# Moving the chain that finds the values' scale from the end of the projections to between the last query blocks

## The chip, the core and the metric

The kernel runs on one core of a Trainium2 chip. A core has a matrix engine (TensorE, PE in the profile), three engines for elementwise work (VectorE or DVE, ScalarE or ACT, GpSimd or POOL) and a queue engine (SyncE or SP) that starts transfers. Each engine takes its instructions in order, and the engines wait for one another at semaphores. The metric is the time of one execution in microseconds (us); lower is better.

## The reference

Two layers of an encoder on 1024 tokens of width 1024. A layer is attention with low-rank queries and values beside a convolution branch, then a gated feed-forward stage:

```python
h = _rmsnorm(x, g_mix[l])
p = h @ w_in[l]
c_q = _rmsnorm(p[..., :o1], g_q[l])
q = (c_q @ w_uq[l]).reshape(b, s, MLA_HEADS, MLA_NOPE_DIM + MLA_ROPE_DIM)
c_kv = _rmsnorm(p[..., o1:o2], g_kv[l])
kv = (c_kv @ w_ukv[l]).reshape(b, s, MLA_HEADS, MLA_NOPE_DIM + MLA_V_DIM)
k_nope, v = kv[..., :MLA_NOPE_DIM], kv[..., MLA_NOPE_DIM:]
y_attn = _mla_attention(q_nope, q_rope, k_nope, k_rope, v)
a, gt = jnp.split(p[..., o3:], 2, axis=-1)
u = jax.nn.silu(_layernorm(_dwconv(a * jax.nn.sigmoid(gt), w_dw_conv[l], b_dw_conv[l]), ...))
x = x + jnp.concatenate([y_attn, u], axis=-1) @ w_o[l]
z = _dwconv(_rmsnorm(x, g_ffn[l]) @ w_up[l], w_dw_ffn[l], b_dw_ffn[l])
zg, zv = jnp.split(z, 2, axis=-1)
x = x + (jax.nn.silu(zg) * zv) @ w_down[l]
```

There are 8 heads with 64 plain and 32 rotary query dimensions and 64 value dimensions. Everything is float32. The kernel splits each float32 operand into an upper and a lower part and multiplies three pairs of parts, so one product of 128 inner rows and 512 columns costs three matmuls.

## The kernel before, in words

A layer has three stages: the projections (`project`), attention (`attention`) and output projection with feed-forward (`feed`). Each stage opens its own pool of PSUM banks, and a bank of the new pool waits for the last reader of the same bank in the old one. The order of the instructions on each engine is written out by hand: what the Python code emits first stands first in the engine's queue.

`project` walks a list `seq` of blocks. For each block n it emits the block's matmuls (`emit`), then VectorE work that the planner has by then (`work`), then what the entry names as `after`, and then it puts the block's eviction on the planner's list (`launch`). The last entries are the query blocks `u0`, `u1` (rotary part) and `n0` to `n3` (plain part), 18 matmuls each, on three wide PSUM tiles in turn. The eviction of block j (`query`, L741 to L745) multiplies the product by the query's norm on VectorE (L741), casts the result to its upper part on ScalarE (L743), and takes the lower part on VectorE (L745); stores on SP's queue then put both parts into memory ("spills"), from which the later heads' operands are loaded again. Head 0 gets its operands straight from these tiles. The value weights `w["v"]` are cast by a transfer on GpSimd's queue; the lower part is made by a copy on ScalarE (L189) and an adding transfer (L190), emitted ahead of `n1`.

Scratch tiles come from a ring of 31 slots: each new tile takes the slot of the oldest, and its writer waits for that tile's last users, transfers among them.

The values are stored as two 16-bit parts, so they need a scale. It is found by a short chain:
- `value_squares`: two ScalarE activations (L860) square the weighted upper value weights, one for each half of the 256 latent rows, and sum each along its row into a column of the small tile `vf`;
- `value_scale`: two matmuls with a matrix of ones (L868) add these columns over the rows into one PSUM tile, and three VectorE operations on a column (L870 to L872) make from the sum's exponent the scale `vs` and its inverse `vr`.

In this kernel `value_squares` is emitted in the return statement of `project`, behind the last eviction, and `value_scale` is the first thing that `attention` emits.

`attention` then emits the value rows: `rows(tt)` makes six matmuls for 128 tokens (L1538), and its eviction makes the upper part on ScalarE (L1548) and the lower on VectorE (L1551), both with `vs`. Three such blocks come first, then scores of query block 0 (L1562), block 3, scores of query block 1, blocks 4 and 5, and then scores of query block 2, which stands where the first of the two score tiles must have been emptied by the exponential (L1572), which needs the maximum from VectorE (L1564). From there each step has scores, transposes of the exponentials (L1602), their eviction (L1604, L1605) and the product with the values (L1625). Beside it GpSimd makes late taps of the convolution (L1794 to L1799) from an agenda by step; at the end it adds up the convolution's channels (L1805), and the first matmul behind the last product with the values is that of the convolution's norm (`lnp`, L1821).

Of the kernel before, what the change touches and what calls it, by code (L numbers as in the profile page):

```python
# [25 lines left out]
QL = 384  # L26
# [99 lines left out]
class Encoder:  # L126
# [421 lines left out]
    def project(self, l, carry):  # L548
# [3 lines left out]
        taps, active, u, conv, away, far_at = [], [], {}, {}, {}, {}  # L552
        gates, ckv, kvs, cq, cqs, vs, w = {}, [], [], [], [], [], {}
        heads, pending, spills = {}, {}, []
        qd = [self.dp.tile([HEADS, NOPE, T], F32R, name=f"qd{l}{i}") for i in range(2)]
        qrd = [self.dp.tile([2, HEADS, HALF, T], F32R, name=f"qrd{l}{i}") for i in range(2)]
        kd = [self.dp.tile([HEADS, NOPE, T], F32R, name=f"kd{l}{i}") for i in range(2)]
        krd = [self.dp.tile([ROPE, T], F32R, name=f"krd{l}{i}") for i in range(2)]
        st = {}

        def work(until):
            while True:
                at = next((e for e in active if e[0] <= clock["dve"]), None)
                if at is None and taps and clock["dve"] + TAP <= until:
                    j, t = taps.pop(0)
                    self.conv_step(l, j, u[j], conv[j], t)
                    clock["dve"] += TAP
                    continue
                if at is None:
                    at = min(active, key=lambda e: e[0], default=None)  # L570
                    if at is None or at[0] > until:
                        return
                    clock["dve"] = max(clock["dve"], at[0])
                step = next(at[1], None)
                if step is None:
                    active.remove(at)
                else:
                    clock["dve"] += step[0]
                    at[0] = clock["dve"] + step[1]

        def launch(steps, n=-1):
            active.append([clock["pe"], steps, n])
# [130 lines left out]
        def query_rope(i):  # L713
            p = ps[f"u{i}"]
            c, s = self.blk(f"rc{l}_{i}"), self.blk(f"rs{l}_{i}")
            nc.vector.tensor_tensor(out=c, in0=p, in1=st["cos"], op=ALU.mult)
            nc.vector.tensor_tensor(out=s, in0=p, in1=st["sin"], op=ALU.mult)
            st["rope", i] = c, s
            yield 2.44, 0.0
            if i == 0:  # L720
                return
            (c1, s1), (c2, s2) = st.pop(("rope", 0)), st.pop(("rope", 1))
            nc.vector.tensor_tensor(out=c1, in0=c1, in1=s2, op=ALU.subtract)
            nc.vector.tensor_tensor(out=c2, in0=c2, in1=s1, op=ALU.add)
            his = [self.blk(f"qr{l}_{i}", F32R) for i in range(2)]
            for hi, o in zip(his, (c1, c2)):
                nc.scalar.copy(out=hi, in_=o)
            yield 2.5, 1.0
            for i, (hi, o) in enumerate(zip(his, (c1, c2))):
                nc.vector.scalar_tensor_tensor(out=o.bitcast(F32R), in0=o, scalar=1.0, in1=hi.bitcast(F32), op0=ALU.mult, op1=ALU.subtract)  # L730
                sp = hi, o.bitcast(F32R)
                yield 1.25, 0.0
                for p in range(2):
                    for h in range(DIRECT):
                        self.move(heads[h][0][p][NOPE + i * HALF:NOPE + (i + 1) * HALF, :],
                                  sp[p][h * HALF:(h + 1) * HALF, :])
                spills.extend((qrd[p][i].rearrange("h d t -> (h d) t"), sp[p]) for p in range(2))

        def query(j):
            n = self.blk(f"qn{l}_{j}")  # L740
            nc.vector.tensor_tensor(out=n, in0=ps[f"n{j}"], in1=st["rq"], op=ALU.mult)  # L741
            hi = self.blk(f"qns{l}_{j}", F32R)
            nc.scalar.copy(out=hi, in_=n)  # L743
            yield 1.22, 1.5
            nc.vector.scalar_tensor_tensor(out=n.bitcast(F32R), in0=n, scalar=1.0, in1=hi.bitcast(F32), op0=ALU.mult, op1=ALU.subtract)  # L745
            sp = hi, n.bitcast(F32R)
            for p in range(2):
                for e in range(DIRECT if j == 0 else 0):
                    self.move(heads[e][0][p][0:NOPE, :], sp[p][e * 64:(e + 1) * 64, :])
                spills.append((qd[p][2 * j:2 * j + 2].rearrange("h d t -> (h d) t"), sp[p]))  # L750
            while j and spills:
                self.move(*spills.pop(0))
            yield 1.25, 0.0
# [11 lines left out]
        def ranked(group, j, n, name, moving):  # L765
            def run():
                pair = tuple(t[:, j] for t in w[group])
                self.product(ps[name], lambda k: tuple(t[:, k * 128:(k + 1) * 128] for t in pair), moving)
            return run
# [20 lines left out]
        add = lambda name, weight, emit, evict, after=None: seq.append((name, weight, emit, evict, after))  # L790
# [19 lines left out]
        for i in range(2):  # L810
            held = lambda: launch(query_rope(0), len(seq) - 6)
            add(f"u{i}", "u2", ranked("u2", i, QL, f"u{i}", cqs), lambda i=i: query_rope(1) if i else iter(()), held if i else norm)
        for j in range(4):
            add(f"n{j}", f"u{j // 2}", ranked(f"u{j // 2}", j % 2, QL, f"n{j}", cqs), lambda j=j: query(j))

        times, starts, t = {}, {}, 0.0
        for name, weight, *_ in seq:
# [33 lines left out]
            launch(evict(), n)  # L851
        supply(clock["pe"])
        work(1e9)
        return u, conv, away, (qd, qrd, kd, krd), (kvs, w["v"], self.value_squares(l, w["v"])), heads

    def value_squares(self, l, w):
        f = self.cp.tile([128, 8], F32, name=f"vf{l}", tag="vf", bufs=1)
# [667 lines left out]
    def attention(self, l, u, conv, away, spill, kvs, loaded, ahead, wo, begun):  # L1525
# [2 lines left out]

        load = lambda h: self.load_head(l, h, *spill)
        state, v, vts = {}, [], {}  # L1530
        vs, vr = self.value_scale(l, kvs[2])

        def rows(tt):
            (kv, wv, _), ts = kvs, slice(tt * 128, (tt + 1) * 128)
# [153 lines left out]
        while any(rest.values()):  # L1688
            j = max((j for j in rest if rest[j]), key=lambda j: (all(j != e for e, _ in late[-2:]), len(rest[j]), -j))
# [3 lines left out]
        for i, (j, t) in enumerate(late):  # L1693
            n, steps = int(SIDE_TIME * sum(costs[:i]) / sum(costs)), self.tap_late(l, j, t, u[j], conv[j], kinds[i])
# [245 lines left out]
```

## Time and profile before

| | us |
|---|---|
| Median of 3 runs | 2290.26 |
| Lowest and highest | 2286.81, 2290.73 |
| Profiled execution, its own time | 2288.28 |
| Its span | 2286.5 |

| Engine | busy us | share of the span |
|---|---|---|
| TensorE | 2269.4 | 99% |
| VectorE | 1735.7 | 76% |
| ScalarE | 1298.6 | 57% |
| GpSimd | 781.9 | 34% |

The profile is one execution. A row of the timeline gives the start and the duration in us, the engine, the line of the kernel, the operation, what it writes and reads, and, in brackets, for how long the engine had been idle before it and whom it waited for. A row marked x6 stands for six instructions in sequence. The chain of work follows the work that ended last backward from its end. A row of waits names who waited for whom, the total in us, the number of times and the longest. A row of windows gives for a stretch of time the length, the busy time and number of instructions of each engine, the clock granted to TensorE (1.00 is full), the share of the transfer engines and GB/s. Lines are those of the kernel before; the change adds two lines above line 815, so later lines count two more after it.

### The profile page before, as it was taken

What the parts mean: (1) busy time and instruction counts of PE and PEld (TensorE: products, weight loads), DVE (VectorE), ACT (ScalarE), POOL (GpSimd) and SP (SyncE); (2) the same over time, 40 slices, a digit from 0 to 9 for tenths busy, and PEclk for the clock granted to TensorE, in tenths of its full rate; (3) what the DMA queues carried; (4) which work ended last, traced back from release to release, by engine and by line L of the source; (5) the groups of instructions that cost most, each with busy time, mean ns of one, the idle gap of its engine ahead of it and who ended that gap; (6) DMA issues with size and microseconds to landing.
All of it is one profiled execution on the core that took longest, in us unless ns stands there. A gap on an engine that the chain in (4) does not pass through costs nothing.

```text
span 2286.5 us, 30445 instructions
## 1 busy us (share of the span) xinstructions
PE 2269.4 (99%) x10690; PEld 1838.8 (80%) x10690; DVE 1735.7 (76%) x2305; ACT 1298.6 (57%) x2058; POOL 781.9 (34%) x812
## 2 busy tenths in 40 slices
PE   9999999999999999999999999999999999999998
PEld 8887777788888888888888877777888888888887
DVE  7988888868877776776559778887687777768765
ACT  5355977646655555544533468785466555555444
POOL 1221788522333333001412237964323333320032
PEclk9999999999999999999999999999999999999999
DMA  6887998846899998935968979977659999988356
GB/s 195 166 181 243 193 205 180 226 133 148 211 279 293 278 295 206 334 106 143 206 137 166 224 224 205 190 157 204 175 122 228 268 303 277 293 213 316 109 120 171
DMA packets 199145, 475.73 MB, mean 208 GB/s; under 512 B 27232, under 2 KB 35280, under 8 KB 198992
## 3 DMA queue, kind: packets, MB, share of 16 engines
q0 software_dynamic: 103136, 222.46, 48.5%
q1 hardware_dynamic: 95568, 250.80, 32.8%
q8 instruction: 84, 1.38, 0.2%
q14 instruction: 69, 0.57, 0.1%
q10 hardware_dynamic: 288, 0.53, 0.1%
HBM read 309.29 MB, written 80.40 MB: 170 GB/s over the span
## 4 chain that ended last, share of the span: by engine, by line
PE 88%; DVE 6%; DMA 2%; ACT 2%; issue 2%; POOL 0%; DVEq 0%; SPq 0%; POOLq 0%; ACTq 0%
PE p L1118 34%; PE pd L1306 18%; PE po L929 7%; PE s L1562 7%; PE t L1602 4%; PE o L1625 4%; PE pa L226 2%; PE pg L226 2%; DVE conv L1777 2%; PE pg L545 2%; PE pq L226 1%; PE pv L1538 1%; PE pkv L226 1%; PE pa L545 1%; PE pn L226 1%
## 5 line engine op out<-in xcount | busy, mean ns | idle before, releaser
L1118 PE MATMUL p<-b,w 128*128 128x512 f32 x3552 | 806.9, 389 | 0.3 <-DVE w L1497 0.2
L1118 PEld LDWEIGHTS p<-b,w 128*128 128x128 f32 x3552 | 666.2, 188 | 140.3 <-DVE w L1497 1.0
L1306 PE MATMUL pd<-ab,wd 128*128 128x512 f32 (+1 forms) x1920 | 422.3, 381 | 0.0
L1306 PEld LDWEIGHTS pd<-ab,wd 128*128 128x128 f32 x1920 | 350.7, 188 | 69.5 <-DVE ab L1497 0.4
L190 POOL DMA_DIRECT2D w<-wu x96 | 84.8, 886 | 360.2 <-ACT w L189 317.7
L1562 PE MATMUL s<-k,q 96*128 96x512 f32 x768 | 207.5, 405 | 0.0
L1605 DVE SCALAR_TENSOR_TENSOR pt<-t,pt 128x512 f16<-128x512 f32 x256 | 164.8, 685 | 38.9 <-ACT pt L1604 38.3
L1794 POOL TENSOR_TENSOR late<-gate,par 128x1014 f32<-128x1014 f32 (+12 forms) x79 | 171.8, 2175 | 15.8 <-DVE qn L741 15.8
L1604 ACT ACTIVATE pt<-t 128x512 f16<-128x512 f32 x256 | 139.2, 595 | 56.6 <-PE t L1602 55.6
L1509 DVE SCALAR_TENSOR_TENSOR o<-zg,par,o 128x1023 f32<-128x1023 f32 x88 | 112.8, 1284 | 75.6 <-ACT o L1503 74.3
L190 POOL DMA_DIRECT2D w<-in_w_up x116 | 100.5, 867 | 199.4 <-ACT w L189 175.3
L1564 DVE TENSOR_REDUCE mx<-s 128x1 f32<-128x1024 f32 x128 | 155.8, 1218 | 1.2 <-PE s L1562 1.2
L1562 PEld LDWEIGHTS s<-k,q 96*128 96x128 f32 x768 | 135.4, 189 | 22.2
L1777 DVE SCALAR_TENSOR_TENSOR conv<-gate,par,conv 128x1009 f32<-128x1009 f32 (+7 forms) x112 | 142.3, 1274 | 3.7 <-ACT conv L607 1.0
L1572 ACT ACTIVATE p<-s,mx 128x1024 f32<-128x1024 f32 x128 | 143.2, 1119 | 1.8 <-DVE mx L1564 1.3
L1602 PEld LDWEIGHTS t<-ident,p 128*128 128x128 f32 x1024 | 119.8, 141 | 25.2 <-DVE yt L1632 0.8
L892 POOL DMA_DIRECT2D wd<-in_w_down x44 | 33.2, 758 | 307.7 <-PE pd L1306 301.8
L1067 DVE TENSOR_TENSOR zg<-p,zg 128x512 f32<-128x512 f32 x88 | 60.6, 690 | 99.3 <-PE p L1118 92.4
L1495 ACT CAST ab<-ac 128x512 fp32r<-128x512 f32 x130 | 80.1, 617 | 97.9 <-DVE ac L1241 95.2
L189 ACT ACTIVATE w<-w 128x512 fp32r<-128x512 f32 x212 | 133.5, 630 | 3.0
L1625 PE MATMUL o<-pt,v 128*128 128x512 f16 x512 | 132.8, 381 | 1.2 <-DVE pt L1605 1.1
L1602 PE MATMUL t<-ident,p 128*128 128x128 f32 x1024 | 133.2, 273 | 0.1
(2117 smaller groups left out, 4090.7 us busy)
## 6 DMA issues: line engine op xcount, KB each, us to landing
w<-in_w_up POOLq DMA_DIRECT2D x232, 256.0 KB, 7.2
wu<-in_w_up SPq DMA_DIRECT2D x88, 512.0 KB, 5.7
w<-wu POOLq DMA_DIRECT2D x96, 256.0 KB, 5.9
sd<-in_w_down SPq DMA_DIRECT2D x44, 512.0 KB, 9.8
ws<-sd SPq DMA_DIRECT2D x44, 512.0 KB, 6.7
wd<-in_w_down POOLq DMA_DIRECT2D x88, 256.0 KB, 5.4
act<-v SPq DMA_DIRECT2D x36, 512.0 KB, 5.8
ac<-act SPq DMA_DIRECT2D x72, 256.0 KB, 6.1
```

What stands on the lines that cost most here:

```text
L190: self.nc.gpsimd.dma_start(out=lo, in_=src, accum_op=ALU.add)
L226: nc.tensor.matmul(ps[:, HALVES[c]], w, x[:, HALVES[c]], start=(k == 0 and s == 0), stop=(k == n - 1 and s == 2))
L929: self.nc.tensor.matmul(ps, p[:, sl], q[:, cs], start=(k == 0 and t == 0), stop=(k == 3 and t == 2))
L1118: nc.tensor.matmul(ps, w[p][:, k * 128:(k + 1) * 128], b[:, q], start=(i in (1, 5, 2) and k == 0 and t == 0), stop=(k == 3 and t == 2), sk ...
L1306: nc.tensor.matmul(ps[t, m][:, cs], w[i, j][p][:, m * 128:(m + 1) * 128], b[:, q, cs], start=(i in (1, 5, 2) and j == 0 and s == 0), stop= ...
L1562: nc.tensor.matmul(ps[:, cs], q[i][0:96, qs], k[j][0:96, cs], start=(s == 0), stop=(s == 2))
L1564: nc.vector.tensor_reduce(out=mx, in_=ps, op=ALU.max, axis=AX.X, negate=True)
L1602: nc.tensor.transpose(tp[:, i, qi * 128:(qi + 1) * 128], st["p"][2 * qp + qi][:, kt * 128:(kt + 1) * 128], self.ident)
L1605: nc.vector.scalar_tensor_tensor(out=lo, in0=tp, scalar=P_SCALE, in1=hi, op0=ALU.mult, op1=ALU.subtract)
L1625: nc.tensor.matmul(po, v[2 * c + i][:, h // 2, e, :], pt[s][:, 2 * (c % 2) + i, :], start=(c == 0 and i == 0 and s == 0), stop=(c == 3 and ...
L1777: self.nc.vector.scalar_tensor_tensor(out=y[:, lo:hi], in0=u[:, lo + s:hi + s], scalar=self.tap(l, j, t), in1=y[:, lo:hi], op0=ALU.mult, o ...
L1794: self.nc.gpsimd.tensor_tensor(out=p[:, lo:hi], in0=u[:, lo + s:hi + s], in1=self.tap(l, j, t).broadcast_to([128, hi - lo]), op=ALU.mult)
```

## The change

The squares are emitted after the matmuls of query block `n1`, ahead of that block's eviction, and the sum with the three small operations after the matmuls of `n2`. The PSUM tile of the sum then comes from the banks of the projections' pool, and attention starts with its four single banks untouched, so its rotation over them is one further back. The tiles that the squares write are taken from the ring before those of blocks 1 to 3 and no longer after them.

```diff
         for i in range(2):
             held = lambda: launch(query_rope(0), len(seq) - 6)
             add(f"u{i}", "u2", ranked("u2", i, QL, f"u{i}", cqs), lambda i=i: query_rope(1) if i else iter(()), held if i else norm)
+        scales = {1: lambda: st.update(squares=self.value_squares(l, w["v"])),
+                  2: lambda: st.update(scale=self.value_scale(l, st.pop("squares")))}
         for j in range(4):
-            add(f"n{j}", f"u{j // 2}", ranked(f"u{j // 2}", j % 2, QL, f"n{j}", cqs), lambda j=j: query(j))
+            add(f"n{j}", f"u{j // 2}", ranked(f"u{j // 2}", j % 2, QL, f"n{j}", cqs), lambda j=j: query(j), scales.get(j))
...
         work(1e9)
-        return u, conv, away, (qd, qrd, kd, krd), (kvs, w["v"], self.value_squares(l, w["v"])), heads
+        return u, conv, away, (qd, qrd, kd, krd), (kvs, w["v"], st["scale"]), heads
...
         state, v, vts = {}, [], {}
-        vs, vr = self.value_scale(l, kvs[2])
+        vs, vr = kvs[2]
```

## The prediction

> **What bounds the kernel now.** I read the waits of TensorE over the whole run first, then the chain of work and the timeline where the long waits are, then the windows for the clock. TensorE is busy for 99% of the span, so the few places where it waits are the whole subject. Of its waits the following are of the matmuls named (total us, times, longest):
>
> ```profile
> PE vf0p L868 <- ACT vsq L860: 4.2, 1, 4.2
> PE vf1p L868 <- ACT vsq L860: 3.1, 1, 3.1
> PE lnp L1821 <- DVE yt L1632: 0.3, 2, 0.2
> PE p L1118 <- DVE w L1497: 0.2, 1, 0.2
> ```
>
> The two longest stand at the same place in the two layers: the matmul over the squares of the value weights, which is what the change moves. The feed-forward stage waits 0.2 us in all, so time won ahead of it is kept. The chain in layer 0 (start, us, what):
>
> ```profile
> 196.77 1.15 DVE qn L741
> ...
> 197.94 1.04 ACT qns L743
> 198.99 1.43 ACT vsq L860 x4
> ...
> 200.46 0.58 PE vf0p L868 x2
> 201.04 6.51 PE pv L1538 x18
> 207.55 1.39 PE s L1562 x6
> 208.94 1.39 PE pv L1538 x6
> ```
>
> The squares (L860) stand in ScalarE's queue behind the cast of the last query block (L743), which waits for VectorE's product (L741), which waits for TensorE: TensorE waits for a chain that starts with its own last matmul. And the 18 matmuls after it take 6.51 us where 6 take 1.39 later on: 18 at that pace are 4.17, so 2.34 us go to a slow clock. The windows show it (third number from the end: granted clock):
>
> ```profile
> 200.90:205.70 4.80, 4.80 (x12) 3.78 (x13) 1.31 (x6) 0.84 (x2) 4.44 (x3) 0.50 1.05 356
> 1334.40:1339.00 4.60, 4.60 (x12) 3.63 (x13) 1.21 (x6) 0.84 (x2) 4.48 (x3) 0.50 1.05 368
> ```
>
> In both layers the half clock follows the idle stretch and ends some 5 us later. The timeline gives the ends of the interval:
>
> ```profile
> 194.97 0.61 PE L226 MATMUL pn<-cqs_2l,wu10h 128*128 128x512 f32 x2
> ...
> 199.75 1.29 PE L868 MATMUL vf0p<-vf,ones 128*128 128x1 f32 x4 [4.17 <-ACT vsq L860]
> ...
> 214.29 1.55 PE L1562 MATMUL s<-k,q 96*128 96x512 f32 x6
> 217.07 1.03 PE L1602 MATMUL t<-ident,p 128*128 128x128 f32 x8
> ```
>
> ```profile
> 1329.59 0.61 PE L226 MATMUL pn<-cqs_2l,wu11h 128*128 128x512 f32 x2
> ...
> 1333.31 1.29 PE L868 MATMUL vf1p<-vf,ones 128*128 128x1 f32 x4 [3.11 <-ACT vsq L860]
> ...
> 1347.70 1.55 PE L1562 MATMUL s<-k,q 96*128 96x512 f32 x6
> ```
>
> From the last query matmul to the third block of scores (214.29, 1347.70) lie eight groups of six matmuls, six of value rows and two of scores. From there on TensorE runs without a gap in layer 0 to 420 us, so what is won by that point passes to the end of attention.
>
> **The change, part by part.** No instruction is added or taken away. The built program's order shows the two squares on ScalarE between the casts of query blocks 0 and 1, the two matmuls on TensorE between the blocks n2 and n3, the three small VectorE operations between the products of blocks 1 and 2; no DMA moves in any queue.
>
> *The squares.* The cast of block 0 is at 188.46 and n3 begins at 191.34:
>
> ```profile
> 188.46 1.03 ACT L743 CAST qns<-qn 128x1024 fp32r<-128x1024 f32 x1
> ...
> 191.34 0.62 PE L226 MATMUL pn<-cqs_0h,wu10h 128*128 128x512 f32 x2
> ```
>
> Squares from 189.5, with 1.43 us, end at 190.9, some 0.4 us before TensorE comes to their matmuls. They take two scratch slots that the last key blocks held; the store that frees them later of the two, and the landings of all these stores (its tile's view), are
>
> ```profile
> 175.86 1.05 SPq L134 DMA_DIRECT2D kd<-kl  x1
> DMA to landing us min/median/max: 3.5/7.1/9.9
> ```
>
> so at the latest about 185.8: no wait. What was queued behind them on ScalarE, the cast of block 1, needs VectorE's product that ends at 192.1 anyway.
>
> *The two matmuls* now run between full ones. At half clock a pair took 0.58; the nearest rows at full clock are the column sums near the end, of the same shape:
>
> ```profile
> L256 PEld LDWEIGHTS rx_768p<-ones,xsq_e x8: 192/192/192, 2278.1 to 2278.8; 128*128 128x128 f32 x8
> ```
>
> Eight in 0.7 to 0.8 us is 0.1 each. The four records (two in each instruction's place) cost 0.4 us; bounds 0.4 and 1.16 (twice 0.58). I take 0.4, since the clock does not fall there.
>
> *TensorE's floor.* In layer 0 the next matmul can issue at 194.97 + 2 x 0.23 = 195.43, plus 0.4, plus 8 x 1.39 = 11.12: third scores at 206.95 instead of 214.29, 7.3 us earlier. In layer 1: 1330.05 + 0.4 + 11.12 = 1341.57 instead of 1347.70, 6.1 earlier. The idle time, the slow clock and the old place of the matmuls are all in these two differences.
>
> *What is late next.* The first exponential must empty its bank before the third scores can start; it needs VectorE:
>
> ```profile
> 194.42 2.36 DVE L745 SCALAR_TENSOR_TENSOR qn<-qn,qns 128x1024 fp32r<-128x1024 f32 x2
> ...
> 197.99 1.89 POOL L1794 TENSOR_TENSOR late<-gate,par 128x1023 f32<-128x1023 f32 x1 [8.29 <-DVE qn L741]
> ...
> 199.02 1.94 DVE L745 SCALAR_TENSOR_TENSOR qn<-qn,qns 128x1024 fp32r<-128x1024 f32 x1 [1.11 <-ACT qns L743]
> ...
> 201.08 0.16 DVE L870 TENSOR_SCALAR vf<-vf0p 128x1 int32<-128x1 int32 x1
> ...
> 201.34 0.14 DVE L872 TENSOR_SCALAR vf<-vf 128x1 int32<-128x1 int32 x1
> ...
> 204.72 0.88 DVE L1551 SCALAR_TENSOR_TENSOR v<-pv,vf,v 128x256 f16<-128x256 f32 x2 [3.23 <-ACT v L1548]
> ...
> 208.46 0.88 DVE L1551 SCALAR_TENSOR_TENSOR v<-pv,vf,v 128x256 f16<-128x256 f32 x2 [0.49 <-ACT v L1548]
> 209.25 1.22 DVE L1564 TENSOR_REDUCE mx<-s 128x1 f32<-128x1024 f32 x1
> ...
> 212.51 1.12 ACT L1572 ACTIVATE p<-s,mx 128x1024 f32<-128x1024 f32 x1
> ```
>
> The three small operations take 0.4 us (201.08 to 201.48) in front of the later products, in a VectorE that had no gap before the last one. The shifted scratch slots also let GpSimd's first late tap start when TensorE has read its last query operand, near 196, not at 197.99. Then it runs beside the lower part of block 2: such an operation takes 1.18 alone and 1.94 beside GpSimd, so 0.76 more. Last product done at 197.92 + 0.4 + 0.76 = 199.1; cast 200.1; its lower part, beside GpSimd as before, 202.1; three pairs of evictions at 0.85, 204.6; maximum 205.8; exponential 206.95. That is the floor's time: a tie, and with hand-overs the third scores at about 207.05. The transposes follow by 1.12 + 1.72 (four value evictions on ScalarE) + 1.12 after 205.85, near 210, instead of 217.07: 7.1 won in layer 0. In layer 1 the last product waits for TensorE and ends near 1331.9, so the exponential ends near 1339.8, 1.8 before it is needed: 6.1 won.
>
> [...]
>
> *The end of attention.* The freed bank turns the rotation by one, and the first matmul behind the last values no longer waits for their eviction:
>
> ```profile
> 423.68 0.40 PE L929 MATMUL po_e<-ys_7h,wo 128*128 128x512 f32 x1
> 424.25 0.50 PE L1821 MATMUL lnp<-lns0h,ones_r 128*128 128x512 f32 x1 [0.17 <-DVE yt L1632]
> ```
>
> It could issue at 423.91; 0.34 won per layer, 0.7 in both (bounds 0 and 0.7).
>
> *Sum:* 7.1 + 6.1 + 0.7 = 13.9 us. The profiled execution took 2288.28 us with a span of 2286.5, 1.98 below the median of 2290.26 and inside the runs' 2286.81 to 2290.73: 2288.28 - 13.9 = 2274.4 us.
>
> **The rivals.** *Head 1 is late.* Its operands are loaded behind the spills in SP's queue, which is full and does not move with TensorE:
>
> ```profile
> 218.19 0.58 SPq L134 DMA_DIRECT2D k<-krd  x1
> DMA to landing us min/median/max: 4.8/5.7/6.7
> 233.30 1.60 PE L1562 MATMUL s<-k,q 96*128 96x512 f32 x6
> ```
>
> The last lands by 224.9 and will be needed at 226.2 instead of 233.30. If spills and loads move back by 4 us, 2.7 us per layer are lost: 2280. Against it: no DMA changes its place.
>
> *GpSimd doesn't follow.* It is nearly full through the late taps; if its end stays where it is, attention's last step waits and the gain is given back: 2288. But it has a pause that ScalarE sets, in step with TensorE,
>
> ```profile
> 401.22 0.91 POOL L190 DMA_DIRECT2D wo<-in_w_o  x1 [8.19 <-ACT pt L1604]
> ```
>
> and 8.19 us of it cover the 7.1.
>
> *The wait comes back in front of n3 (the other side).* TensorE takes its matmuls in order: if the squares end late, the whole of n3 stands behind them. Each us past 191.3 costs one, and after a pause like layer 1's 3.11 the slow clock's 2.3 come on top; from 4.7 us late (4.7 + 2.3 is half of 13.9) a layer loses more than it wins. With 7 us late in both layers: 2 x (7 + 2.3) - 13.9 = 4.7 slower, 2293. For that the squares would have to start near 197, so the slots' stores to land there instead of by 185.8.
>
> **How the numbers follow.** My forecast has 0.80. Its own bounds: matmuls at 1.16, 1.5 less; VectorE stretched everywhere, 4 less; the bank's turn worth nothing, 0.7 less; not all together, so a gain of 9.8 to 14.4, which with the runs' scatter of 2 us is 2272 to 2281. Head 1 late or GpSimd in part behind: 0.11, 2279 to 2286. Gain all given back: 0.05. The wait in front of n3: 0.04. A change of 0.2% (4.6 us) is about what a measurement can tell here. Faster 0.90, same 0.06, slower 0.04; the range 2271 to 2284 leaves out the last two and the far half of the second.
>
> **What would show it.** Right: the wait for the squares gone from TensorE's list, the clock at 1.00 throughout the first value rows, third scores near 207 and 1341.6, the two small matmuls 0.4 us before n3. Wrong: a new wait before n3, before the third scores or before head 1's first scores, or an lnp wait grown by microseconds.

## The result and the profile after

| | before | after |
|---|---|---|
| median, us | 2289.85 (6 runs) | 2276.66 (6 runs) |
| lowest and highest | 2286.81, 2290.73 | 2275.48, 2280.34 |
| profiled execution, its own time | 2288.28 | 2276.63 |
| its span | 2286.5 | 2274.9 |
| mean granted clock of TensorE | 0.997 | 0.999 |

The changed kernel takes 0.9948 of the time of before (95% interval 0.9935 to 0.9961). Between the two profiled executions 11.6 us of span are won, where the prediction's sum was 13.9. The medians of this table differ by 13.2 us, but the kernel before had medians of 2288.1 to 2288.6 in the later runs, and beside those the change wins 11.8.

The waits of TensorE for the squares are gone. What is left of its waits in the changed kernel (total us, times, longest), beside two of 1.1 us and one of 0.2 that both kernels have:

```profile
PE pv L1540 <- DVE v L1553: 0.9, 1, 0.9
PE s L1564 <- ACT p L1574: 0.8, 1, 0.8
PE p L1120 <- DVE zv L1069: 0.5, 1, 0.5
```

The first two are new, and both stand in the start of attention of layer 0. The windows of the changed kernel (third number from the end: granted clock) answer to the two windows at 0.50 of before:

```profile
195.50:200.00 4.50, 4.50 (x21) 3.59 (x21) 4.24 (x3) 0.17 (x1) 4.13 (x3) 1.00 1.01 356
200.00:205.00 5.00, 4.22 (x19) 3.10 (x17) 4.08 (x4) 4.98 (x10) 3.02 (x2) 1.00 1.05 309
1324.00:1330.00 6.00, 6.00 (x28) 4.99 (x27) 4.46 (x4) 2.89 (x6) 4.10 (x3) 1.00 1.02 352
```

The clock stays full. In layer 1 the chain of work runs through the value rows with no wait, 18 matmuls in 4.08 us:

```profile
1321.71 4.25 PE pn L226 x18
1325.96 4.08 PE pv L1540 x18
1330.04 1.39 PE s L1564 x6
```

Both programs issue the same matmuls, so the start of each in one trace can be set against its start in the other. The difference, after less before, at a few of them (worked out from the two traces; minus is earlier; "by matched matmuls" below means this comparison):

| matmul | before | after | difference, us |
|---|---|---|---|
| last of the first 18 value matmuls, layer 0 | 205.74 | 198.26 | -7.48 |
| first of the fourth value block | 211.55 | 205.12 | -6.43 |
| third scores | 214.29 | 208.96 | -5.33 |
| lnp, layer 0 | 424.59 | 418.95 | -5.64 |
| feed-forward, layer 0 | 756.49 | 751.59 | -4.89 |
| last of n2, layer 1 | 1325.73 | 1320.99 | -4.74 |
| last of the first 18 value matmuls, layer 1 | 1339.19 | 1328.29 | -10.89 |
| lnp, layer 1 | 1557.69 | 1546.46 | -11.22 |
| last | 2280.65 | 2269.18 | -11.47 |

So TensorE had won what was forecast by its first value rows in layer 0, and then gave back 2.15 us in two steps, 1.05 before the fourth value block and 1.10 before the third scores. Behind lnp 0.90 of it was lost by the end of n2 in layer 1, nearly all in the feed-forward stage of layer 0. Layer 1 won 6.15 us and kept them. The timeline of the changed kernel shows the two steps in layer 0:

```profile
189.22 0.72 ACT L862 ACTIVATE vsq<-wv0h,par 128x512 f32<-128x512 f32 x1
...
191.18 0.50 PE L870 MATMUL vf0p<-vf,ones 128*128 128x1 f32 x4
191.54 0.72 PE L226 MATMUL pn<-cqs_0h,wu10h 128*128 128x512 f32 x2
...
194.56 4.05 DVE L745 SCALAR_TENSOR_TENSOR qn<-qn,qns 128x1024 fp32r<-128x1024 f32 x2
195.57 1.96 POOL L1796 TENSOR_TENSOR late<-gate,par 128x1023 f32<-128x1023 f32 x1 [6.04 <-PE pn L226]
...
200.71 2.39 POOL L1799 TENSOR_TENSOR conv<-conv,late 128x1020 f32<-128x1020 f32 x1
200.92 3.27 DVE L745 SCALAR_TENSOR_TENSOR qn<-qn,qns 128x1024 fp32r<-128x1024 f32 x1 [1.18 <-ACT qns L743]
...
205.12 0.47 PE L1540 MATMUL pv<-wv0h,kvs_0h 128*128 128x512 f32 x1 [0.90 <-DVE v L1553]
...
208.96 1.65 PE L1564 MATMUL s<-k,q 96*128 96x512 f32 x6 [0.84 <-ACT p L1574]
...
211.84 1.04 PE L1604 MATMUL t<-ident,p 128*128 128x128 f32 x8
```

The squares start at 189.22, their matmuls stand without a wait ahead of n3 and cost 0.36 us (191.18 to 191.54), close to the forecast. But VectorE's two lower parts (L745) from 194.56 take 4.05 us where two took 2.36 before, and the last one takes 3.27 where it took 1.94. Two such operations take 2.36 us, and the pair ends at 198.61, 1.08 after GpSimd's tap ends at 197.53. The last one ends at 204.19, 1.09 after GpSimd's sum ends at 203.10. So each of the two that met GpSimd ended about one undisturbed duration after GpSimd's instruction did: it looks as if it waited for the end of that instruction. That is the first thing to test.

### The profile page after: what moved, and what is told of

Read it like the earlier page. It is cut to its first block, busy times and chain, and to the rows that moved or that the text cites. A ratio compares the mean times of both kernels' runs of the same rounds, so it can differ in the third digit from the quotient of the medians.

```text
span 2274.9 us, 30440 instructions
## 1 busy us (share of the span) xinstructions
PE 2264.2 (100%) x10690; PEld 1834.8 (81%) x10690; DVE 1738.7 (76%) x2305; ACT 1298.0 (57%) x2058; POOL 783.0 (34%) x812
## 4 chain that ended last, share of the span: by engine, by line
PE 93%; issue 2%; DVE 2%; DMA 1%; ACT 1%; SPq 0%; POOL 0%; DVEq 0%; POOLq 0%; ACTq 0%
PE p L1120 36%; PE pd L1308 18%; PE po L931 7%; PE s L1564 7%; PE t L1604 4%; PE o L1627 4%; PE pq L226 3%; PE pa L226 3%; PE pkv L226 2%; PE pg L226 2%; PE pg L545 2%; PE pa L545 1%; PE pk L226 1%; PE pn L226 1%; PE pkr L759 1%
```

## The experiments

"Held" below means that GpSimd's first late taps wait until VectorE has done the lower part of query block 3.

| kernel | median, us | runs | before beside it |
|---|---|---|---|
| after_again (the change) | 2276.28 | 2275.81 to 2278.80 | 2288.09 |
| pool_held | 2274.07 | 2273.57 to 2274.59 | 2288.09 |
| squares_only | 2277.45 | 2276.98 to 2279.09 | 2288.09 |
| gap_filled | 2285.73 | 2283.64 to 2288.11 | 2288.09 |
| scale_23 | 2279.13 | 2278.77 to 2280.00 | 2288.62 |
| scale_22 | 2281.95 | 2280.66 to 2285.04 | 2288.62 |
| bank_turned | 2276.47 | 2275.05 to 2276.88 | 2288.62 |
| squares_held | 2274.98 | 2273.62 to 2275.58 | 2288.39 |
| before_held | 2288.05 | 2286.63 to 2290.97 | 2288.39 |
| bank_used | 2278.67 | 2278.11 to 2280.08 | 2288.39 |
| gap_filled_more | 2284.44 | 2283.52 to 2285.83 | 2288.39 |

### The changed kernel once more

> The changed kernel once more, as the measure for the runs beside it. What is open in it: attention of layer 0 lost 2.15 us of the 7.5 that TensorE had won by its first value rows (1.05 in front of the fourth value block, 1.10 in front of the third scores), and the feed-forward stage of layer 0 lost 1.25 us (0.74 of it at 751.6, behind a weight load that landed late). Theory: the first loss is in the order of the instructions and comes back in every run, in the same place and within 0.1 us; the second is the chance of one transfer and changes. Rival: both come back alike, and the change has made the load late. About 2276.7 us.

Measured: 2276.28 us, 0.9952 of before (0.994 to 0.9965). Its third scores lie 2.15 us behind what its first value rows had won, as in the first profile: from 166 to 535 us no matmul moved by more than 0.25 us relative to the rest of that stretch in the other profile of the change. In the feed-forward stage TensorE waited 0.9 us in two places, where the first profile has 0.5 in one; against that profile it is 0.79 us later at 536.7 and has 0.62 of it back at 752.4. So the first loss repeats in place and size, and the second moves about. (The 1.25 us that the expectation gives to the feed-forward stage was read at the first matmul of n3 in layer 1 and holds 0.36 of that layer's own moved matmuls: 0.90 is the stage's.)

### GpSimd held until VectorE has done its part

```diff
...
             while j and spills:
                 self.move(*spills.pop(0))
+            if j == 3:
+                nc.gpsimd.tensor_copy(out=self.cp.tile([128, 1], F32, name=f"hold{l}", tag="held", bufs=1), in_=n[:, 0:1])
             yield 1.25, 0.0
```

The edit also gives an older copy of this kind, at the start of the first layer, the same one-slot tile tag.

> GpSimd's first late taps may start only when VectorE has done the lower part of query block 3 (a copy of one column of that tile stands ahead of them on GpSimd's queue). Theory A: in the changed kernel VectorE's lower parts, with two inputs in SBUF, are held until a GpSimd instruction that runs has ended (a lower part from 195.69 ended at 198.61, GpSimd's tap at 197.52; the last one from 200.92 ended at 204.19, GpSimd's sum at 203.10). Then all three lower parts of blocks 1 to 3 take 1.2 us, the last ends near 200.3, TensorE waits neither in front of the fourth value block (0.90) nor of the third scores (0.84), which stand near 206.9 instead of 208.96, and layer 0 wins 1.9 to 2.1 us more. GpSimd has 18.57 us of waiting behind these taps and loses nothing. Layer 1 has no such wait of TensorE and stays as it is. Together 2274.6 us against some 2276.7. Theory B: the waits come from the order on VectorE alone (three small operations ahead of its products): then they stay and the time is the same. [...]

Measured: 2274.07 us, 0.994 of before (0.9927 to 0.9954), and every one of its five runs is below every one of the change's. The timeline of this kernel:

```profile
195.29 2.35 DVE L745 SCALAR_TENSOR_TENSOR qn<-qn,qns 128x1024 fp32r<-128x1024 f32 x2
199.95 1.23 DVE L745 SCALAR_TENSOR_TENSOR qn<-qn,qns 128x1024 fp32r<-128x1024 f32 x1 [1.17 <-ACT qns L743]
...
201.31 0.18 POOL L754 COPY hold<-qn 128x1 f32<-128x1 f32 x1 [11.05 <-DVE qn L745]
201.53 1.89 POOL L1798 TENSOR_TENSOR late<-gate,par 128x1023 f32<-128x1023 f32 x1
...
207.45 1.55 PE L1566 MATMUL s<-k,q 96*128 96x512 f32 x6
```

The lower parts take 2.35 for two and 1.23 again, and both waits of TensorE are gone. By matched matmuls this kernel gains 1.06 us before the fourth value block and 1.10 before the third scores on the change, 2.16 where 1.9 to 2.1 was expected and just what the change had lost. (Its profile is 0.65 us later from 166 us on, ahead of all this, which is why the scores stand at 207.45 and not at 206.9.) Theory A holds, and this kernel is faster than the kernel before and the change.

### The disputed cost by itself

This program leaves out the layers and runs the disputed operations alone, one block for each pair of them; `both` is the lower part with two inputs in SBUF, `psum` the same with one of them in PSUM, `one` a maximum over a tile in SBUF, `add` and `mult` GpSimd's sum and tap:

```diff
+        part(both, 8, None, 0)
+        part(None, 0, add, 4)
+        part(None, 0, mult, 4)
+        part(both, 8, add, 4)
+        part(both, 8, mult, 4)
+        part(psum, 8, add, 4)
+        part(one, 8, add, 4)
...
```

> Not the reference's computation: only the disputed cost. VectorE runs eight operations in a row, GpSimd four, on tiles of 128x1024 float32, first each alone, then at the same time: lower parts with two inputs in SBUF beside sums and beside taps of GpSimd, then the same with one input in PSUM, then maxima with one input in SBUF. Theory A (the one waits for the whole instruction of the other): a lower part takes 1.2 us alone, a sum 2.4, and beside each other the two engines' busy work doesn't overlap: eight lower parts and four sums take the sum of both, near 19 us, with single lower parts of up to 3.6 us; the forms with one input in SBUF take the same as alone. Theory B (they share the way, each slowed by a factor, 1.94/1.18 = 1.64): every lower part beside a sum takes near 1.9 us, and both together take some 12 to 15 us.

Measured, in the timeline of this program:

```profile
6.25 10.04 DVE L1886 SCALAR_TENSOR_TENSOR o<-x,q 128x1024 f32<-128x1024 f32 x8 [6.25 <-ACT q L1903]
...
17.51 9.58 POOL L1897 TENSOR_TENSOR conv<-conv,q 128x1024 f32<-128x1024 f32 x4 [17.07 <-ACT q L1903]
...
28.25 7.80 POOL L1900 TENSOR_TENSOR late<-g,q 128x1024 f32<-128x1024 f32 x4 [1.16 <-ACT q L1903]
...
37.16 18.12 DVE L1886 SCALAR_TENSOR_TENSOR o<-x,q 128x1024 f32<-128x1024 f32 x8 [20.87 <-ACT q L1903]
37.20 13.22 POOL L1897 TENSOR_TENSOR conv<-conv,q 128x1024 f32<-128x1024 f32 x4 [1.15 <-ACT q L1903]
...
56.46 16.33 DVE L1886 SCALAR_TENSOR_TENSOR o<-x,q 128x1024 f32<-128x1024 f32 x8 [1.19 <-ACT q L1903]
...
73.98 10.03 DVE L1889 SCALAR_TENSOR_TENSOR o<-pv,q 128x1024 f32<-128x1024 f32 x8 [1.19 <-ACT q L1903]
74.03 9.62 POOL L1897 TENSOR_TENSOR conv<-conv,q 128x1024 f32<-128x1024 f32 x4 [6.09 <-ACT q L1903]
...
85.20 10.00 DVE L1892 TENSOR_REDUCE mx<-q 128x1 f32<-128x1024 f32 x8 [1.19 <-ACT q L1903]
85.25 9.62 POOL L1897 TENSOR_TENSOR conv<-conv,q 128x1024 f32<-128x1024 f32 x4 [1.60 <-ACT q L1903]
...
96.39 10.03 DVE L1889 SCALAR_TENSOR_TENSOR o<-pv,q 128x1024 f32<-128x1024 f32 x8 [1.19 <-ACT q L1903]
```

The line's own view gives the shortest, the median and the longest lower part in ns:

```profile
L1886 DVE SCALAR_TENSOR_TENSOR o<-x,q x24: 1224/1226/3245, 6.2 to 71.6; 128x1024 f32<-128x1024 f32 x24
```

Alone, eight lower parts take 10.04 us and four sums 9.58. Together they take 18.12, close to 19.62, the two laid end to end: while both run they take turns, a sum every 3.28 us, and a lower part that has to wait takes up to 3.25. With taps it is the same: four take 7.80 alone, and eight lower parts beside them 16.33, close to 17.84. With one input in PSUM, or with only one input, VectorE takes 10.03 (10.03 alone too, at 96.39) and 10.00 beside the same sums, and GpSimd 9.62: neither is slowed by the other. Theory A holds but for the 1.5 us that the two did overlap (19.62 less 18.12).

### Only the squares early

Set against the change:

```diff
-        scales = {1: lambda: st.update(squares=self.value_squares(l, w["v"])),
-                  2: lambda: st.update(scale=self.value_scale(l, st.pop("squares")))}
+        scales = {1: lambda: st.update(squares=self.value_squares(l, w["v"]))}
...
-        return u, conv, away, (qd, qrd, kd, krd), (kvs, w["v"], st["scale"]), heads
+        return u, conv, away, (qd, qrd, kd, krd), (kvs, w["v"], st["squares"]), heads
...
-        vs, vr = kvs[2]
+        vs, vr = self.value_scale(l, kvs[2])
```

> Of the change only the squares are made early; the sum's two matmuls and the three small operations stay where they were, first in attention. Theory A (ScalarE's queue was the wait): TensorE no longer waits 4.17 and 3.11 us for the squares, the clock stays at 1.00, and what is left is that the small operations stand behind the last lower part on VectorE and ScalarE's value evictions wait for them: 2 to 4 us of the 13.2 lost, so 2278.5 to 2281. Theory B (the place of the matmuls is the main thing): most of the gain is gone, 2286 or more.

Measured: 2277.45 us, 1.2 behind the change, a smaller loss than either theory had. The squares alone bring nearly all of the gain: their matmuls, now at 195.4 without a wait, and the full clock (1.00 in its windows). In layer 0 the third scores are as early as with the whole change (5.50 against 5.33 us earlier than before). What the small operations lose by their old place is seen in the timeline of this kernel:

```profile
199.06 3.64 DVE L745 SCALAR_TENSOR_TENSOR qn<-qn,qns 128x1024 fp32r<-128x1024 f32 x1 [1.17 <-ACT qns L743]
...
199.42 2.19 POOL L1795 TENSOR_TENSOR late<-gate,par 128x1020 f32<-128x1020 f32 x1
...
202.62 0.14 DVE L871 TENSOR_SCALAR vf<-vf0p 128x1 int32<-128x1 int32 x1
...
202.82 0.50 PE L1539 MATMUL pv<-wv0h,kvs_0h 128*128 128x512 f32 x1 [1.29 <-DVE vf L871]
```

The lower part waits for GpSimd here too (202.70 is 1.09 after 201.61), and TensorE waits 1.29 us behind it for the bank of the sum. The expectation set the losses of the old place against the full gain and left out that the change itself loses 2.15 us to GpSimd.

### Only the squares early, and GpSimd held

> Only the squares are early, and GpSimd's first taps are held until the lower part of query block 3 is done, as in pool_held. With squares_only (2277.45), pool_held (2274.07) and the change (2276.28) this fills the square of the two parts. Theory A (of the change the squares are what counts; the place of the sum and the small operations is worth the 0.3 us in front of lnp in each layer and little else once GpSimd is out of the way): no wait of TensorE for VectorE's small operations (1.3 in squares_only), third scores of layer 0 within 0.4 us of pool_held's, 0.6 to 1.2 us behind it in all, 2274.7 to 2275.5. Theory B (the small operations behind the last lower part hold up ScalarE's value evictions by themselves): TensorE still waits about 1 us at the fourth value block or the third scores of layer 0, 2276 or more.

Measured: 2274.98 us, 0.9 behind pool_held, inside the 0.6 to 1.2 of theory A: the wait of 1.29 us is gone. The one wait that pool_held lacks in these places is the one in front of lnp:

```profile
PE lnp L1824 <- DVE yt L1635: 0.4, 2, 0.2
```

With the two kernels above this gives the parts: with GpSimd free 2277.45 with the squares alone and 2276.28 with the sum too, with GpSimd held 2274.98 and 2274.07. The place of the sum is worth about 1 us of some 12 by the medians, though the single runs overlap; GpSimd's start is worth 2.2 to 2.5.

### The kernel before, with GpSimd held

> The kernel before with GpSimd's first taps held until the lower part of query block 3 is done: the lower part takes 1.2 us, not 1.94. Theory A (in the kernel before VectorE was not what TensorE waited for: the squares stood on ScalarE): same as before within 0.1%, the waits of 4.17 and 3.11 us and the half clock stay. Theory B (GpSimd's taps were already part of the price before): 0.7 us or more per layer won, 2286.5 or less beside a before of about 2288.

Measured: 2288.05 us beside 2288.39, 0.9999 of it (0.9989 to 1.0008). The lower part took 1.23 us. TensorE still waits 4.2 us in layer 0 and 3.4 in layer 1 for the squares, and the half clock is there in both layers, in layer 1 for 3.41 us instead of 6.83. The collision with GpSimd costs nothing as long as the squares are what TensorE waits for; the change brought it onto the path.

### The waiting stretch filled with work

In the kernel before, ahead of the two matmuls of the sum and into the same bank:

```diff
...
+        for k in range(14):
+            nc.tensor.matmul(ps, fill[:, 0:128], fill[:, 0:512], start=True, stop=True)
...
```

> The kernel before, with 14 further full matmuls (3.2 us at 0.23 each, on operands that are there, into the sum's own bank, which the sum then overwrites) ahead of the sum's two matmuls in each layer, where TensorE waited 4.17 and 3.11 us for the squares. They are more work than before. Theory A (the half clock comes from the idle stretch): the wait for the squares shrinks to about 1 us in layer 0 and none in layer 1, the clock is 1.00 through the value rows, their first 18 matmuls take 4.2 instead of 6.5 us, and the kernel is 2.3 to 3.2 us per layer faster than before: 2284 to 2286. Theory B (the half clock belongs to the place, whatever TensorE did before): no gain, 2290 or more.

Measured: 2285.73 us, 0.9988 of before (0.9979 to 0.9997), the upper end of what theory A expected. In layer 1 it came out whole: TensorE waits 0.3 us, the clock stays at 1.00, and the first 18 value matmuls win 2.2 us. In layer 0 they win only 0.8 us. The windows of this kernel from 198.88 on are

```profile
198.88:202.29 3.41, 2.06 (x11) 1.42 (x10) 2.23 (x4) 2.28 (x5) 3.11 (x3) 1.00 1.03 418
202.29:205.70 3.41, 3.41 (x10) 2.64 (x9) 0.88 (x2) 0.84 (x2) 3.33 (x2) 0.50 1.05 374
```

A wait of 1.03 and one of 0.32 us were left, with two short matmuls of one column between and behind them, and the clock fell to 0.50 for 3.41 us.

### The same with 18 matmuls in layer 0

```diff
-        for k in range(14):
+        for k in range((18, 14)[l]):
```

> The kernel before with 18 instead of 14 further matmuls in the waiting stretch of layer 0 (14 in layer 1, as in gap_filled). In gap_filled TensorE still waited 1.03 and 0.32 us in layer 0, and the clock fell to 0.50 for one stretch of 3.41 us; in layer 1 it waited 0.32 us and the clock stayed. Theory A (how much TensorE did in the stretch before decides on the clock): with some 0.4 us of waiting left the clock is 1.00 throughout layer 0 too, its first 18 value matmuls take 4.2 us, and 1.3 to 1.7 us more are won than in gap_filled (2285.73): 2284 to 2284.5. Theory B (layer 0 falls whatever is done): half clock there as in gap_filled, 2285.7.

Measured: 2284.44 us, 0.9983 of before (0.9974 to 0.9992), 1.3 less than gap_filled, with more work in it. Each layer keeps one wait of 0.3 us, and the windows stay full:

```profile
199.50:203.00 3.50, 3.08 (x15) 2.24 (x15) 2.23 (x4) 2.11 (x5) 3.20 (x3) 1.00 1.03 417
203.00:206.00 3.00, 3.00 (x15) 2.47 (x14) 1.05 (x3) 1.68 (x4) 2.92 (x2) 1.00 1.06 382
```

So the half clock belongs to the idle stretch and not to the place, and with the short matmuls that ran under it it was 3.95 us of the gain (2288.39 less 2284.44), 2.0 per layer. By matched matmuls of the two profiles it was 2.5 and 2.3, of which this execution had lost 1.2 ahead of attention. The rest of the change's 12 us is for the most part the waiting itself, 4.17 and 3.11 us.

### The chain one block later

```diff
-        scales = {1: lambda: st.update(squares=self.value_squares(l, w["v"])),
-                  2: lambda: st.update(scale=self.value_scale(l, st.pop("squares")))}
+        scales = {2: lambda: st.update(squares=self.value_squares(l, w["v"])),
+                  3: lambda: st.update(scale=self.value_scale(l, st.pop("squares")))}
```

> The chain one query block later than in the change: squares behind the cast of block 1, the two matmuls behind n3, which is the last query block. Theory A (the order on VectorE and GpSimd's start decide in layer 0): TensorE doesn't wait for the squares (cast of block 1 until 193.1, squares until 194.6, n3 ends at 195.4), and the clock stays at 1.00; but the three small operations now wait on VectorE for the sum at some 195.8 with one tap of the convolution and two lower parts behind them, which in the changed kernel started at 193.3: VectorE is some 2.5 us later, it meets more of GpSimd's taps, and the third scores of layer 0 stand 2 to 3.5 us later than 208.96; layer 1 has about 1.8 us of room and loses 0 to 1. Together 2278.5 to 2281. Theory B (only the wait for the squares counts): the same time as the change, 2276.5.

Measured: 2279.13 us, in the range of theory A. The timeline of this kernel:

```profile
195.58 0.50 PE L870 MATMUL vf0p<-vf,ones 128*128 128x1 f32 x4
...
196.12 0.16 DVE L872 TENSOR_SCALAR vf<-vf0p 128x1 int32<-128x1 int32 x1 [2.66 <-PE vf0p L870]
...
197.81 4.54 DVE L745 SCALAR_TENSOR_TENSOR qn<-qn,qns 128x1024 fp32r<-128x1024 f32 x2
...
202.28 1.21 DVE L741 TENSOR_TENSOR qn<-pn,rq 128x1024 f32<-128x1024 f32 x1
...
203.59 2.73 PE L1564 MATMUL s<-k,q 96*128 96x512 f32 x6 [3.26 <-issue]
```

TensorE doesn't wait for the squares, but VectorE waits 2.66 us for the sum, with a tap of the convolution and two lower parts behind it in its queue, and then meets more of GpSimd's taps. The product of block 3 (L741) is done only at 203.49, and the first scores, which need its bank, stand 0.1 behind it, 3.26 us late, at half clock (2.73 us for six), which theory A had not expected. The third scores are 3.17 us behind the change. The profile names no releaser for the 3.26; that it is L741 follows from the bank and the times.

### The whole chain in front of n3

```diff
-        scales = {1: lambda: st.update(squares=self.value_squares(l, w["v"])),
-                  2: lambda: st.update(scale=self.value_scale(l, st.pop("squares")))}
+        scales = {2: lambda: st.update(scale=self.value_scale(l, self.value_squares(l, w["v"])))}
```

> The whole chain behind query block n2: the squares stand behind the cast of block 1 on ScalarE (which ends near 193.1), the two matmuls in front of n3 as in the change. This makes the wait in front of n3 that the prediction had as its rival. Theory A (its price there: a us for each us late, and 2.3 us of slow clock on top after a pause of over 3 us): squares end near 194.6, n3 begins near 195.0 instead of 191.5, 3.5 us of idle TensorE and 2.3 of slow clock in layer 0, in layer 1 somewhat less: 4 to 6 us per layer, 2285 to 2288, where the kernel before stands. Theory B (n3's products are not needed so early, VectorE and GpSimd bound the start of attention anyway): less than half of that, under 2282.

Measured: 2281.95 us, below theory A's range and at the edge of theory B's. It makes the wait that the prediction's third rival was about:

```profile
PE vf0p L869 <- ACT vsq L861: 2.9, 2, 2.5
PE vf1p L869 <- ACT vsq L861: 1.5, 2, 1.2
```

On TensorE alone the price in layer 0 is near the rival's: by matched matmuls 3.3 us up to the sum and 1.6 more by a half clock from 196.16 to 199.58, 4.9 in all. Of these 2.2 come back, since the two waits for VectorE in the changed kernel (1.05 and 1.10 by matched matmuls) vanish when TensorE is later; GpSimd, too, starts later here. So layer 0 loses 2.7. In layer 1 the squares are only 1.5 us late, the clock stays, and 1.9 are lost. The rival's rule was right for TensorE and left out what a later TensorE saves elsewhere.

### The turn of the banks

```diff
         vs, vr = kvs[2]
+        self.bank(f"turn{l}")
```

> The change with one single bank taken and not used at the start of attention, so that the rotation of the four banks is that of the kernel before again. Theory A (the prediction's last term): the wait of the lnp matmul for the last eviction is back, 0.15 to 0.2 us in each layer, and the gain of 0.3 per layer that the milestone showed goes: 0.6 us more, 2277 us. In layer 0 the fourth value block, too, then takes another bank. Theory B: the lnp wait comes from the end of attention as a whole, and no wait returns.

Measured: 2276.47 us and no wait in front of lnp. The experiment failed: a tile that nothing uses takes no bank, and the program is the change's own, instruction for instruction. It counts as one more run of the change.

```diff
         vs, vr = kvs[2]
+        nc.tensor.matmul(self.bank(f"turn{l}", (128, 1)), self.ones, self.ones[:, 0:1], start=True, stop=True)
```

> The change with one single bank taken by one matmul of a column at the start of attention (0.1 us of TensorE), which restores the banks that the later tiles had in the kernel before; the unused tile of bank_turned took no bank. Theory A (the prediction's last term): the wait for the last eviction in front of lnp is back, 0.15 to 0.2 us in each layer, and the milestone behind it is 0.3 us later than in the change; 0.6 to 0.8 us in all. Theory B: no wait, no difference.

Measured: the wait in front of lnp is back, 0.2 us in each layer, and by matched matmuls 0.3 to 0.5 us go there in each layer. The median, 2278.67, is 2.4 behind the change and not 0.6 to 0.8; in its profile 1.5 us are lost to the change's by the last matmul, of which 0.7 stand in the feed-forward stage of layer 1. That surplus isn't explained by the bank, and whether it is scatter can't be told from three runs.

## Why the prediction was right, and where it wasn't

The forecast was 2274.4 us, within 2271 to 2284; 2276.66 was measured. Its mechanism is the one that the runs show: the squares in ScalarE's queue were the wait, and the half clock followed from it. The start of the sum mattered as much as its terms: taken from the median of three runs, 2290.26, and not from the profiled 2288.28, the same 13.9 would have given 2276.4, nearly the measured time, but by luck, since the later runs have the kernel before at 2288.1 to 2288.6 and the gain at 11.8. Point by point:

- *The squares.* As forecast: 189.22 to 190.73, TensorE at their matmuls at 191.18, no wait for a slot.
- *The two matmuls.* 0.36 us up to the first matmul of n3 against 0.4, and 0.5 with the first matmuls of n3, which follow a little slower (layer 0 goes from -0.16 to 0.35, layer 1 from -4.74 to -4.24); the bound of 1.16 was far off.
- *TensorE's floor.* Layer 1 came out at 6.15 us by matched matmuls (-4.74 to -10.89) against 6.1. Layer 0 had 7.5 by the value rows against 7.3. The slow clock's share of these numbers is shown by gap_filled_more, 2.0 us per layer by the medians and 2.3 to 2.5 by matched matmuls, against the 2.34 of the prediction.
- *What is late next.* This is the step that failed. It saw the place (VectorE's lower parts beside GpSimd's taps, in layer 0 only, a tie with the floor) but priced the new collision at 0.76 us and the old one as unchanged. The 0.76 was read from one row, 1.94 against 1.18, as if such an operation beside GpSimd took a fixed time. In that row GpSimd's tap ran from 197.99 to 199.88 and the lower part from 199.02: it had met only the last 0.86 us of the tap. The price was about what was left of GpSimd's instruction: 1.69 in the pair and 2.05 in the last one (3.27 less 1.22). This took 2.15 us of TensorE's 7.5, and left 5.3 of the 7.1 that the sum had for layer 0: 1.8 of the 2.4 us by which the sum was too high at the last matmul. pool_held shows the cause, since with GpSimd out of the way the 2.16 come back, and port_price shows it on the operations alone, 18.12 us where the two laid end to end are 19.62.
- *The bound on VectorE.* The forecast's bounds have 4 us for a VectorE stretched everywhere. No run shows that term. Beside GpSimd's sums the lower parts, with two inputs in SBUF, took longer (18.12 us for eight in port_price, 10.04 alone), and those with one input in PSUM didn't (10.03), nor the maxima (10.00); in the kernel before a pair of evictions with one input in PSUM took 0.88 at 204.72, where GpSimd's sum runs from 203.06 for 2.36, and 0.88 at 208.46 without it. What the lower parts lost cost TensorE 2.15 us in layer 0 and none in layer 1, in place of the 4.
- *The end of attention.* 0.31 and 0.33 us against 0.34 per layer. squares_only, squares_held and bank_used, which leave the banks unturned, all have the wait, 0.4 us in two places together.
- *The feed-forward stage.* The prediction's "time won ahead of it is kept" was too simple: layer 0 lost 0.9 us there in this profile. TensorE's waits in that stage, from the profiles of all these kernels, are 0 to 1.0 us; both kernels with early squares and a held GpSimd have none, the other kernels with early squares 0.3 to 1.0, and those with late squares 0.2 to 1.0. Behind the one of 0.5 stands a weight load that landed late. Whether the change makes it likelier is open.

The sum as it came out by matched matmuls: 5.33 + 6.15 + 0.64 for the three terms, less 0.90 for layer 0's feed-forward stage, and 0.25 more behind layer 1's lnp: 11.47. The feed-forward stage is a term that the sum put at nothing.

The rivals: head 1 wasn't late (no wait of TensorE for its scores), GpSimd followed, and no wait stood in front of n3. That wait, made on purpose in scale_22, cost 5.7 us against after_again.

## What to carry to other kernels

Where a long wait goes, find the engine that is in a tie behind it and ask what it collides with at its new time. A row of a stretched operation is no price until one has seen how much of the other operation it overlapped: in these runs a lower part with two inputs in SBUF lost about what was left of the GpSimd sum or tap that ran (1.69 and 2.05 us in the change; 18.12 us in port_price, where the two end to end are 19.62), and one with an input in PSUM nothing (10.03 beside four sums, 10.03 alone). GpSimd work with slack behind it (18.57 us here) could be held by a copy of one column that depends on the right tile, which cost 0.18 us and won 2.2 in pool_held.

## What the runs showed of the hardware that was not expected

Around the start of attention the granted clock fell and came back in stretches of 3.41 us or twice that. The windows of the kernel before, cut at the edges of its clock records:

```profile
195.57:198.98 3.41, 0.01 (x1) 0.00 (x0) 2.34 (x3) 1.04 (x2) 0.99 (x1) 1.00 1.00 333
198.98:205.81 6.83, 5.94 (x16) 4.79 (x17) 3.19 (x6) 2.27 (x7) 6.06 (x4) 0.50 1.05 371
```

The half clock lasted 6.83 us there and in layer 1, and 3.41 us in gap_filled, scale_22, scale_23 and layer 1 of before_held, so one or two stretches of 3.41. Its starts in the two layers of the kernel before, 198.98 and 1332.21, lie 1133.23 us apart, 332 times 3.4133, with the clock at 1.00 from 205.81 to the second: as far as these two show, the stretches kept their beat through all that TensorE did between. It began 0.8 and 1.3 us after TensorE was at work again (gap_filled: value rows from 201.46, half clock from 202.29; scale_22: n3 from 194.84, half clock from 196.16), so it came with the end of the stretch that held the wait, not with the wait itself. And no long pause was needed: in gap_filled it followed 1.35 us of waiting, with a busy share of 2.06 in 3.41, in scale_22's layer 0 1.94 in 3.41. The same 1.5 us of waiting left the clock alone in scale_22's layer 1, as did a single wait of 1.29 us in squares_only. Between the edges that the clock records of these two kernels give, the stretches that hold these waits (in scale_22 all but 0.2 us of it) are, squares_only first,

```profile
200.29:203.70 3.41, 2.12 (x10) 1.42 (x9) 2.69 (x4) 0.65 (x2) 3.33 (x2) 1.00 1.04 371
1322.56:1325.97 3.41, 2.08 (x10) 1.38 (x8) 1.03 (x1) 2.35 (x5) 0.00 (x0) 1.00 0.99 160
```

They are hardly busier than the 2.06 us of gap_filled. It is clearer to count the full matmuls (512 columns) that start in a stretch; at 0.23 us each, 15 fit. Around the start of attention half clock followed stretches with none and four (layer 0 of the kernel before), five and three (its layer 1), five (gap_filled) and six (scale_22's layer 0), and full clock followed stretches with six (the one of scale_22 above), eight (squares_only) and, in both layers of the kernel before, eight. The count alone doesn't settle it: six stands on both sides, and near the end of the kernel before full clock followed a stretch with 28 short matmuls and no full one (2277.70 to 2281.11, TensorE busy for 3.22 us of it). As far as these show, it matters where a wait falls in the stretches; where the border lies is shown no closer.

GpSimd waited for VectorE as well: in layer 1 of the changed kernel

```profile
1328.40 3.27 DVE L745 SCALAR_TENSOR_TENSOR qn<-qn,qns 128x1024 fp32r<-128x1024 f32 x1 [1.17 <-ACT qns L743]
...
1330.65 3.25 POOL L1799 TENSOR_TENSOR conv<-conv,late 128x1019 f32<-128x1019 f32 x1
```

VectorE's lower part ends at 1331.67, and GpSimd's sum, recorded from 1330.65, takes 3.25 us where it took 2.36 before: so a recorded start can be that of the wait, on either engine. Who goes first can't be read from the recorded starts: in squares_only the lower part is recorded 0.36 us ahead of GpSimd's tap and still ended 1.09 behind it.
